# A convolution layer on Trainium2: kept low weight parts, seven taps from GpSimd to VectorE, and bias tables by three products instead of twelve

## The chip, the cores and the metric

The kernel runs on one core of a Trainium2 chip. Engines are named as in the profile: PE is TensorE, DVE is VectorE, ACT is ScalarE, POOL is GpSimd, SP is SyncE, whose queue issues most DMAs. The metric is the device time of one execution in microseconds (us), as the median of several runs.

## What is computed

A trunk of a convolution layer and an attention layer, each followed by a dense SwiGLU FFN, on 1024 tokens with 1024 channels in float32. The change lies in the convolution layer and in the table of position biases that attention uses later:

```
u = h @ w_pw1 + b_pw1
a, gate = split(u, 2)
u = a * sigmoid(gate)
u = depthwise_conv(u, w_dw, width 31, causal) + b_dw
u = silu(layernorm(u, ln_g, ln_b))
out = u @ w_pw2 + b_pw2
...
bias = bias_table[t5_bucket(dist * dilation)]
```

## The kernel before

The tokens are worked on in two halves of 512, h0 and h1. Channels lie on partitions, in eight chunks c of 128, so a tile is 128 x 512. Products in float32 are made of three products of rounded parts: `gemm` multiplies high weight by high data (L155), low weight by high data (L156) and high weight by low data (L157), eight times three matmuls for a tile. A tile is divided by `split`: ACT casts it to its high part (L127), and DVE or POOL subtracts that from it to get the low part (L128).

`conv_and_half_ffn` runs the convolution layer and the first FFN's half. `pw1_weights(c)` loads the two weight tiles of chunk c from `w1` (two DMAs of 512 KB on SP) and splits them. `glu(h, c)` makes the two products of the gate (L155 to L157), the sigmoid on ACT (L367) and the gated tile u on DVE (L374). The first half takes all eight chunks; chunks 5 to 7 do the second half too with the same weights. The chunks 0 to 4 of the second half load and split their weights again: 0 to 3 ahead of the convolution's end, 4 behind the layernorm in the program's text.

`conv(0)` is the convolution of width 31 for h0. A pair of chunks has 31 taps: `POOL_TAPS` of them are multiplied by ACT (L403, into the buffers m, of which there are two) and summed by POOL (L404), the rest are multiplied and summed by DVE into a bank of PSUM (L410, L412); a last addition on DVE joins the two (L422). The weights of the second half, the splits of L128 and the taps share DVE, POOL and ACT.

`layernorm(0)` follows: column sums on PE over the eight chunks (L434), subtraction of the mean on DVE (L436), squares on ACT (L457) and their column sums on PE (L458), square root on ACT (L460), reciprocal on DVE (L464), eight scalings on DVE (L468), Silu on ACT (L470), and a split into the pair y. `pw2` multiplies y by `w2`, whose eight weight tiles come through `weights` (DMA at L140), and adds into x. Then come the norm and the FFN of h0; the convolution of h1 runs beside that FFN and waits for its norm.

`bias_rows` makes the bias tables of the twelve heads: three groups of four. For each group a one-hot table is loaded (L603), and for each head one product on PE (L607) spreads its row over 128 partitions, ACT negates it (L609) and stores 192 KB to the memory `scratch` on its own queue (L610). Attention reads `scratch` much later, at about 1100 us.

The order of the instructions on each engine is found by the framework's scheduler from the program's order and its own model; what an engine does next is fixed when the kernel is built.

Of the kernel before, what the change touches and what calls it, by code (L numbers as in the profile page):

```python
# [17 lines left out]
P = 128  # L18
T = 1024
TH = 512  # L20
D = 1024
# [23 lines left out]

POOL_TAPS = ((11, 14, 15, 15), (10, 10, 9, 9))

# [38 lines left out]
@with_exitstack  # L86
def trunk(ctx, tc, xT, vecs, wdw, w1, w2, wqkv, wo, wg, wu, wd, rel, onehot, sel, outT, scratch):
    nc = tc.nc
# [49 lines left out]
    def weights(ap, n=D, into=None):  # L138
# [8 lines left out]
        return wh, wl  # L147

    def gemm(ps, w, xs, kt=DC, off=0):

        wh, wl = w
        for k in range(kt):
            sl = slice(off + k * P, off + (k + 1) * P)
            xh, xl = xs(k)
            nc.tensor.matmul(ps, wh[:, sl], xh, start=(k == 0), stop=False)  # L155
            nc.tensor.matmul(ps, wl[:, sl], xh, start=False, stop=False)  # L156
            nc.tensor.matmul(ps, wh[:, sl], xl, start=False, stop=(k == kt - 1))  # L157

# [13 lines left out]
    main = Scratch(tpool, "tmp", tpool, "ssq", aux_ps)  # L172


    marks = {}

# [142 lines left out]
    def conv_and_half_ffn():  # L319

        with ExitStack() as cs:
# [12 lines left out]

            def pw1_weights(c):

                t = slot([P, 2, 2, D])
                for i in range(2):
                    pw1_part(t, c, i, staging(), slice(0, D))
                return pw1_pairs(t)  # L340

            def staging():
# [8 lines left out]
            def pw1_pairs(t):  # L351
                return [(t[:, i, 0], t[:, i, 1]) for i in range(2)]

            def glu(h, c, hl, bc=None, w=None):

                wb, wa = w or pw1_weights(c)
                pb = mm_ps()
# [66 lines left out]
            def layernorm(h, sl, y):  # L424
# [42 lines left out]
                for c in range(DC):  # L467
                    nc.vector.tensor_tensor(out=vs[c], in0=vs[c], in1=br, op=ALU.mult)  # L468
                    t = sc.tmp()[:, :n]
                    nc.scalar.activation(  # L470
                        t,
                        vs[c],
                        AF.Silu,
                        bias=vec[:, V_LNB + c : V_LNB + c + 1],
                        scale=vec[:, V_LNG + c : V_LNG + c + 1],
                    )
                    split(t, yh[:, c, sl], yl[:, c, sl], nc.vector if c % 2 else nc.gpsimd)

# [40 lines left out]
            for c in range(DC):  # L519
                w = pw1_weights(c) if c else pw1_pairs(first)  # L520
                glu(0, c, ha, bc, w)
                if c == 0:
                    nc.sync.dma_start(wd_sb, wdw)
                if c in (1, 2):
                    for i in range(4):
                        load_x(1, (c - 1) * 4 + i)
                if c == NORM_B:
                    rms_into(hb, 1, V_MIX, sc=nsc)
                if c >= JOINT:
                    glu(1, c, hb, w=w)  # L530
# [7 lines left out]
            layernorm(0, whole, y)  # L538
            bias_rows()
            for c in range(LATE[0], LATE[1]):  # L540
                glu(1, c, hb)
            pw2(0, whole, y)
            for c in range(LATE[1], JOINT):
# [51 lines left out]
    def bias_rows():  # L595
# [5 lines left out]
        for g in range(NG):  # L601
            oh = tmp()[: NBK + 1, : 3 * P]
            nc.sync.dma_start(oh, onehot[g])  # L603
            for h in range(HPG):
                c = g * HPG + h
                ps = aux_ps()[:, : 3 * P]
                nc.tensor.matmul(ps, rb[:, c : c + 1].broadcast_to([NBK + 1, P]), oh, start=True, stop=True)  # L607
                br = tmp()[:, : 3 * P]
                nc.scalar.mul(br, ps, -1.0)  # L609
                nc.scalar.dma_start(scratch[g, h], br)  # L610

# [711 lines left out]
```

## Time and profile before

| | us |
|---|---|
| median of 3 runs | 2151.76 |
| runs | 2149.31, 2153.92, 2151.76 |
| the profiled execution | 2155.0 |
| its span in the trace | 2153.0 |
| PE busy | 2090.3 (97%) |
| DVE busy | 1361.7 (63%) |
| ACT busy | 845.2 (39%) |
| POOL busy | 550.0 (26%) |

Busy time is the time in which an engine works on an instruction. A share over the whole span is a mean of stages that have different limits, so it does not say what sets the time in a stage; the timeline of a stretch and what ended an engine's idle time do. The granted clock is a share of TensorE's full speed.

### The profile page before, as it was taken

How to read it: one execution, taken by the hardware profiler on the slowest of the kernel's cores; microseconds unless marked ns; L12 is line 12 of the kernel's file. 1: busy time of each engine (PE TensorE's matmuls, PEld its weight loads, DVE VectorE, ACT ScalarE, POOL GpSimd, SP SyncE). 2: the span in 40 equal slices, each digit the busy share in tenths (PEclk: the TensorE clock that was granted, in tenths of full speed). 3: DMA queues.
4: the chain of work that ended last, by engine and by line, in shares of the span. 5: the costliest groups of instructions: out<-in, count | busy, mean ns of one | idle time of the engine just before them, and what ended most of it. 6: DMA issues, size and time to landing. Idle time of an engine off the chain costs nothing.

```text
span 2153.0 us, 24602 instructions
## 1 busy us (share of the span) xinstructions
PE 2090.3 (97%) x9568; PEld 1686.9 (78%) x9568; DVE 1361.7 (63%) x1979; ACT 845.2 (39%) x1362; POOL 550.0 (26%) x336
## 2 busy tenths in 40 slices
PE   8998889999999999999999999999999999999997
PEld 6786578778887888888887777777888888888887
DVE  8998577998545433332562437489866666666665
ACT  6765656523423222212353434455322222222234
POOL 2998159922322222211231112130000000000003
PEclk9999989999999999999999999999999999999999
DMA  6111222223232222221231212112111111111112
GB/s 238 59 40 50 85 69 89 79 98 98 89 98 91 97 96 98 98 88 49 71 116 59 69 54 67 45 62 88 60 59 59 50 49 59 49 50 40 59 59 79
DMA packets 51320, 162.12 MB, mean 75 GB/s; under 512 B 5885, under 2 KB 11268, under 8 KB 51204
## 3 DMA queue, kind: packets, MB, share of 16 engines
q1 hardware_dynamic: 48900, 157.67, 22.2%
q10 hardware_dynamic: 2304, 2.88, 0.4%
q8 instruction: 75, 1.23, 0.2%
q14 instruction: 41, 0.34, 0.1%
HBM read 153.98 MB, written 6.55 MB: 75 GB/s over the span
## 4 chain that ended last, share of the span: by engine, by line
PE 76%; DVE 10%; POOL 9%; issue 3%; ACT 2%; DMA 1%; SPq 0%; POOLq 0%; DVEq 0%; ACTq 0%
PE mm L155 11%; PE mm L156 11%; PE mm L157 11%; POOL ap L404 7%; PE aux L155 6%; PE aux L156 6%; PE aux L157 6%; PE mm L1003 4%; PE mm L1001 4%; PE mm L1002 4%; DVE cacc L412 3%; PE nps L1001 2%; PE nps L1002 2%; PE nps L1003 2%; DVE slot L128 2%
## 5 line engine op out<-in xcount | busy, mean ns | idle before, releaser
L155 PE MATMUL mm<-slot,wh 128*128 128x512 f32 x1184 | 467.5, 395 | 5.3 <-DVE u L374 3.7
L156 PE MATMUL mm<-slot,wl 128*128 128x512 f32 x1184 | 466.4, 394 | 2.6 <-DVE wl L128 2.5
L157 PE MATMUL mm<-slot,wh 128*128 128x512 f32 x1184 | 464.0, 394 | 1.3 <-DVE slot L128 1.3
L128 POOL TENSOR_TENSOR wl<-ws,wh 128x1024 fp32r<-128x1024 f32 (+1 forms) x91 | 215.4, 2368 | 792.5 <-ACT wh L127 761.3
L127 ACT CAST wh<-ws 128x1024 fp32r<-128x1024 f32 (+1 forms) x190 | 195.6, 1030 | 337.2 <-PE mm L157 160.9
L155 PEld LDWEIGHTS mm<-slot,wh 128*128 128x128 f32 x1184 | 224.6, 190 | 57.5 <-issue 7.6
L156 PEld LDWEIGHTS mm<-slot,wl 128*128 128x128 f32 x1184 | 224.5, 190 | 51.9 <-DVE wl L128 3.8
L157 PEld LDWEIGHTS mm<-slot,wh 128*128 128x128 f32 x1184 | 224.0, 189 | 49.8 <-DVE slot L128 1.7
L404 POOL TENSOR_TENSOR ap<-ap,m 128x512 f32<-128x512 f32 x170 | 247.9, 1492 | 46.6 <-ACT m L403 46.6
L128 DVE TENSOR_TENSOR wl<-ws,wh 128x1024 fp32r<-128x1024 f32 (+1 forms) x99 | 131.5, 1329 | 151.1 <-ACT wh L127 150.9
L412 DVE SCALAR_TENSOR_TENSOR cacc<-u,wd_sb,cacc 128x512 f32<-128x512 f32 x288 | 198.8, 744 | 0.1
L128 POOL TENSOR_TENSOR slot<-ws,slot 128x1024 fp32r<-128x1024 f32 x2 | 4.8, 2407 | 638.9 <-ACT slot L127 638.9
L403 ACT ACTIVATE m<-u,wd_sb 128x512 f32<-128x512 f32 x170 | 121.6, 723 | 91.0 <-POOL ap L404 90.7
L155 PE MATMUL aux<-slot,wh 128*128 128x512 f32 x352 | 139.1, 395 | 7.7 <-DVE x L316 7.7
L1001 PE MATMUL mm<-slot,wp 128*128 128x512 f32 x352 | 137.6, 391 | 3.0 <-ACT wp L127 1.6
L156 PE MATMUL aux<-slot,wl 128*128 128x512 f32 x352 | 138.5, 393 | 0.8 <-DVE wl L128 0.5
L157 PE MATMUL aux<-slot,wh 128*128 128x512 f32 x352 | 138.4, 393 | 0.0
L1002 PE MATMUL mm<-slot,wp 128*128 128x512 f32 x352 | 137.6, 391 | 0.0
L1003 PE MATMUL mm<-slot,wp 128*128 128x512 f32 x352 | 137.0, 391 | 0.0
L127 ACT CAST wp<-ws 128x512 fp32r<-128x512 f32 x110 | 67.9, 620 | 142.2 <-PE mm L1003 58.2
L918 DVE TENSOR_TENSOR x<-aux,x 128x512 f32<-128x512 f32 x144 | 98.7, 688 | 35.3 <-PE aux L157 34.4
L128 DVE TENSOR_TENSOR slot<-tmp,slot 128x512 fp32r<-128x512 f32 x58 | 96.0, 1658 | 28.7 <-ACT slot L127 28.4
(269 smaller groups left out, 3820.4 us busy)
## 6 DMA issues: line engine op xcount, KB each, us to landing
ws<-wd SPq DMA_DIRECT2D x66, 512.0 KB, 3.5
ws<-wu SPq DMA_DIRECT2D x64, 512.0 KB, 3.5
ws<-wg SPq DMA_DIRECT2D x62, 512.0 KB, 3.5
ws<-w SPq DMA_DIRECT2D x40, 512.0 KB, 3.6
ws<-wqkv SPq DMA_DIRECT2D x34, 512.0 KB, 3.5
ws<-wo SPq DMA_DIRECT2D x16, 384.0 KB, 3.1
x<-xT SPq DMA_DIRECT2D x16, 256.0 KB, 6.3
scratch<-tmp ACTq DMA_DIRECT2D x12, 192.0 KB, 1.9
```

The lines of the kernel that those rows point to most:

```text
L127: a = nc.scalar.copy(hi, src)
L128: b = eng.tensor_tensor(out=lo, in0=src, in1=hi.bitcast(F32), op=ALU.subtract)
L155: nc.tensor.matmul(ps, wh[:, sl], xh, start=(k == 0), stop=False)
L156: nc.tensor.matmul(ps, wl[:, sl], xh, start=False, stop=False)
L157: nc.tensor.matmul(ps, wh[:, sl], xl, start=False, stop=(k == kt - 1))
L403: nc.scalar.activation(m, src(c, k), AF.Copy, scale=wk)
L404: nc.gpsimd.tensor_tensor(out=a, in0=a, in1=m, op=ALU.add)
L412: nc.vector.scalar_tensor_tensor(out=a if k or late else u[h, c][:, :TH], in0=src(c, k), scalar=wk, in1=b if k == nv - 1 else a, op0=ALU.mult,
L918: eng.tensor_tensor(out=out, in0=a, in1=b, op=op)
L1001: nc.tensor.matmul(ps, wh, xh, start=start and k == 0, stop=False, skip_group_check=not start)
L1002: nc.tensor.matmul(ps, wl, xh, start=False, stop=False, skip_group_check=not start)
L1003: nc.tensor.matmul(ps, wh, xl, start=False, stop=k == 3, skip_group_check=not start)
```

## The change

Four things change in `conv_and_half_ffn` and `bias_rows`.

- `POOL_TAPS` for h0 goes from (11, 14, 15, 15) to (11, 13, 12, 12) per pair of chunks: seven taps of two chunks, so fourteen products on ACT and sums on POOL, become fourteen instructions on DVE.
- A memory tensor `kept1` takes the low parts of the weights of chunks 0 to 4 (ten stores of 512 KB on SP). For h1 these chunks load the weight again, cast it on ACT, and load the low part from `kept1` and cast it on ACT too; the subtraction on DVE is gone there.
- In the layernorm of h0 the high part of y is a copy on DVE instead of a cast on ACT; the low part is a subtraction on DVE or POOL as before.
- `bias_rows` may start when the last product of glu(1, 4) is done. One product per group makes the rows of four heads, 32 partitions each, with a table `heads` that DVE writes first (one copy per group); DVE negates the result (three times); each head's 32 partitions go out four times, 48 KB each, on SP's queue: 48 stores.

```
@@ -43,7 +43,7 @@
 SKEW = 3 * P - 1
 
 
-POOL_TAPS = ((11, 14, 15, 15), (10, 10, 9, 9))
+POOL_TAPS = ((11, 13, 12, 12), (10, 10, 9, 9))
 
 
 LATE_SUM = ((0, 1, 2, 3), (0,))
@@ -154,7 +157,8 @@
             xh, xl = xs(k)
             nc.tensor.matmul(ps, wh[:, sl], xh, start=(k == 0), stop=False)
             nc.tensor.matmul(ps, wl[:, sl], xh, start=False, stop=False)
-            nc.tensor.matmul(ps, wh[:, sl], xl, start=False, stop=(k == kt - 1))
+            mm = nc.tensor.matmul(ps, wh[:, sl], xl, start=False, stop=(k == kt - 1))
+        marks["gemm"] = mm.ins
 
     def pairs(hl, sl=slice(None)):
         hi, lo = hl
@@ -332,12 +333,26 @@
             stage = ("ws", "ws", "wh", "wl", "wh", "wl", "wh", "wl")
             staged = [0]
 
-            def pw1_weights(c):
+            def pw1_weights(c, again=False):
+
 
                 t = slot([P, 2, 2, D])
                 for i in range(2):
-                    pw1_part(t, c, i, staging(), slice(0, D))
+                    ws = staging()
+                    if again:
+                        nc.sync.dma_start(ws, w1[c if i else DC + c])
+                        nc.scalar.copy(t[:, i, 0], ws)
+                        lo = staging()
+                        nc.sync.dma_start(lo, kept1[c, i])
+                        nc.scalar.copy(t[:, i, 1], lo)
+                    else:
+                        pw1_part(t, c, i, ws, slice(0, D))
+                        if c < JOINT:
+                            pw1_keep(t, c, i)
                 return pw1_pairs(t)
+
+            def pw1_keep(t, c, i):
+                nc.sync.dma_start(kept1[c, i], t[:, i, 1].bitcast(F32))
 
             def staging():
                 tag = stage[staged[0] % len(stage)]
@@ -353,7 +368,7 @@
 
             def glu(h, c, hl, bc=None, w=None):
 
-                wb, wa = w or pw1_weights(c)
+                wb, wa = w or pw1_weights(c, True)
                 pb = mm_ps()
                 gemm(pb, wb, pairs(hl))
                 pa = mm_ps()
@@ -474,7 +489,12 @@
                         bias=vec[:, V_LNB + c : V_LNB + c + 1],
                         scale=vec[:, V_LNG + c : V_LNG + c + 1],
                     )
-                    split(t, yh[:, c, sl], yl[:, c, sl], nc.vector if c % 2 else nc.gpsimd)
+                    if h == 0:
+                        nc.vector.tensor_copy(yh[:, c, sl], t)
+                        eng = nc.vector if c % 2 else nc.gpsimd
+                        eng.tensor_tensor(out=yl[:, c, sl], in0=t, in1=yh[:, c, sl].bitcast(F32), op=ALU.subtract)
+                    else:
+                        split(t, yh[:, c, sl], yl[:, c, sl], nc.vector if c % 2 else nc.gpsimd)
 
             def pw2(h, sl, y):
                 for d in range(DC):
@@ -520,6 +540,8 @@
                 w = pw1_weights(c) if c else pw1_pairs(first)
                 glu(0, c, ha, bc, w)
                 if c == 0:
+                    pw1_keep(first, 0, 0)
+                    pw1_keep(first, 0, 1)
                     nc.sync.dma_start(wd_sb, wdw)
                 if c in (1, 2):
                     for i in range(4):
@@ -536,9 +558,10 @@
                     touch(y)
             conv(0, range(4))
             layernorm(0, whole, y)
-            bias_rows()
             for c in range(LATE[0], LATE[1]):
                 glu(1, c, hb)
+            with tc.issue_after(marks["gemm"]):
+                bias_rows()
             pw2(0, whole, y)
             for c in range(LATE[1], JOINT):
                 glu(1, c, hb)
@@ -599,15 +622,20 @@
         nc.vector.memset(rb, 1.0)
         nc.sync.dma_start(rb[:NBK], rel)
         for g in range(NG):
-            oh = tmp()[: NBK + 1, : 3 * P]
+            both = tmp()[: NBK + 1]
+            oh, heads = both[:, : 3 * P], both[:, 3 * P :]
             nc.sync.dma_start(oh, onehot[g])
+
+            cols = rb[:, g * HPG : (g + 1) * HPG].unsqueeze(2).broadcast_to([NBK + 1, HPG, P // HPG])
+            nc.vector.tensor_copy(heads.rearrange("p (h r) -> p h r", h=HPG), cols)
+            ps = aux_ps()[:, : 3 * P]
+            nc.tensor.matmul(ps, heads, oh, start=True, stop=True)
+            br = tmp()[:, : 3 * P]
+            nc.vector.tensor_scalar(out=br, in0=ps, scalar1=-1.0, scalar2=None, op0=ALU.mult)
             for h in range(HPG):
-                c = g * HPG + h
-                ps = aux_ps()[:, : 3 * P]
-                nc.tensor.matmul(ps, rb[:, c : c + 1].broadcast_to([NBK + 1, P]), oh, start=True, stop=True)
-                br = tmp()[:, : 3 * P]
-                nc.scalar.mul(br, ps, -1.0)
-                nc.scalar.dma_start(scratch[g, h], br)
+                for i in range(HPG):
+                    n = P // HPG
+                    nc.sync.dma_start(scratch[g, h, i * n : (i + 1) * n], br[h * n : (h + 1) * n])
 
     def toeplitz(apool, g):
 
```

On PE, at the end of the layernorm's squares. L458, now L473, is the column sum of the squares; L607, now L632, the product of the biases; slot and wh, wl are the operands of pw2. Before:

```order
L458 MATMUL aux<-ctmp,ones 128x512
L607 MATMUL aux<-tmp,vec 128x384
L458 MATMUL aux<-ctmp,ones 128x512 x2
L607 MATMUL aux<-tmp,vec 128x384
L458 MATMUL aux<-ctmp,ones 128x512
L607 MATMUL aux<-tmp,vec 128x384
L458 MATMUL aux<-ctmp,ones 128x512
L607 MATMUL aux<-tmp,vec 128x384
L458 MATMUL aux<-ctmp,ones 128x512 x2
L607 MATMUL aux<-tmp,vec 128x384 x2
L458 MATMUL aux<-ctmp,ones 128x512
L607 MATMUL aux<-tmp,vec 128x384 x6
```

The change:

```order
L473 MATMUL aux<-ctmp,ones 128x512
L632 MATMUL aux<-tmp 128x384
L473 MATMUL aux<-ctmp,ones 128x512 x2
L632 MATMUL aux<-tmp 128x384
L473 MATMUL aux<-ctmp,ones 128x512 x5
L158 MATMUL mm<-slot,wh 128x512
L159 MATMUL mm<-slot,wl 128x512
L158 MATMUL mm<-slot,wh 128x512
L159 MATMUL mm<-slot,wl 128x512
L632 MATMUL aux<-tmp 128x384
```

Twelve bias products have become three; the third of them stands behind the first four products of pw2. All products of the last projection, glu(1, 4), are now ahead of these rows, and 32 of their 48 ahead of the last column sum of L449 (L434 before).

On DVE, behind the squares. L464 and L468, now L479 and L483, are reciprocal and scaling; L374, now L389, is the gated product of glu(1, 4); L630 writes the table of heads and L634 negates the result; L493 and L495 are high and low part of y. Before:

```order
L422 TENSOR_TENSOR u<-cacc,ap 128x512 x2
L436 SCALAR_TENSOR_TENSOR u<-aux,u 128x512 x8
L464 RECIPROCAL csv<-csv 128x512
L468 TENSOR_TENSOR u<-u,csv 128x512 x8
L374 SCALAR_TENSOR_TENSOR u<-mm,vec,tmp 128x512
L128 TENSOR_TENSOR slot<-ctmp,slot 128x512
L374 SCALAR_TENSOR_TENSOR u<-mm,vec,tmp 128x512
L128 TENSOR_TENSOR slot<-ctmp,slot 128x512 x3
```

The change:

```order
L634 TENSOR_SCALAR tmp<-aux 128x384
L630 COPY tmp<-vec 33x128
L634 TENSOR_SCALAR tmp<-aux 128x384
L479 RECIPROCAL csv<-csv 128x512
L630 COPY tmp<-vec 33x128
L483 TENSOR_TENSOR u<-u,csv 128x512 x8
L389 SCALAR_TENSOR_TENSOR u<-mm,vec,tmp 128x512
L493 CAST slot<-ctmp 128x512 x2
L389 SCALAR_TENSOR_TENSOR u<-mm,vec,tmp 128x512
L495 TENSOR_TENSOR slot<-ctmp,slot 128x512
L493 CAST slot<-ctmp 128x512 x2
L634 TENSOR_SCALAR tmp<-aux 128x384
```

The scalings stand together as before, but behind the third copy of heads, which writes into a buffer that the stores of the first group's rows read; the copies of y stand between the last negations and the gate.

On SP, from the weights of pw2 on. L140 loads those weights, L627 a one-hot table, L638 stores bias rows:

```order
L140 DMA ws<-w 128x1024 x5
L627 DMA tmp<-onehot 33x384 x2
L638 DMA scratch<-tmp 32x384 x32
L627 DMA tmp<-onehot 33x384
L638 DMA scratch<-tmp 32x384 x16
L140 DMA ws<-w 128x1024 x3
```

The stores of a group stand behind its negation on DVE, and the third group's one-hot table behind 32 of them; before, the stores were on ACT's queue. The loads of the last three weight tiles of pw2 come behind all 48.

## Rows read from the trace of the kernel before

**Rows 1.** Page: busy time by engine, the chain by engine and by line.
```profile
PE 2090.3 (97%) x9568; PEld 1686.9 (78%) x9568; DVE 1361.7 (63%) x1979; ACT 845.2 (39%) x1362; POOL 550.0 (26%) x336
...
PE 76%; DVE 10%; POOL 9%; issue 3%; ACT 2%; DMA 1%; SPq 0%; POOLq 0%; DVEq 0%; ACTq 0%
PE mm L155 11%; PE mm L156 11%; PE mm L157 11%; POOL ap L404 7%; PE aux L155 6%; PE aux L156 6%; PE aux L157 6%; PE mm L1003 4%; PE mm L1001 4%; PE mm L1002 4%; DVE cacc L412 3%; PE nps L1001 2%; PE nps L1002 2%; PE nps L1003 2%; DVE slot L128 2%
```

**Rows 2.** Windows: stretch, length, busy us of PE, PEld, DVE, ACT, POOL, clock, DMA, GB/s.
```profile
144.00:200.00 56.00, 55.97 (x240) 44.67 (x239) 53.59 (x69) 38.52 (x56) 51.80 (x36) 1.00 0.09 30
200.00:207.00 7.00, 0.55 (x3) 0.12 (x1) 5.36 (x7) 3.73 (x5) 7.00 (x6) 0.82 0.38 141
207.00:213.00 6.00, 5.38 (x12) 3.34 (x13) 1.94 (x4) 0.00 (x0) 1.06 (x1) 0.64 0.03 13
213.00:239.00 26.00, 19.83 (x44) 7.49 (x44) 14.60 (x19) 18.62 (x33) 1.76 (x1) 0.86 0.26 95
```

**Rows 3.** Waits of PE: us in total, times, longest.
```profile
PE aux L434 <- DVE u L422: 7.1, 1, 7.1
```

**Rows 4.** Timeline of POOL: start, length, line, count, idle before and its releaser.
```profile
139.52 5.52 POOL L404 TENSOR_TENSOR ap<-ap,m 128x512 f32<-128x512 f32 x4
...
189.11 18.96 POOL L404 TENSOR_TENSOR ap<-ap,m 128x512 f32<-128x512 f32 x12 [0.84 <-ACT m L403]
```

**Rows 5.** Timeline of DVE, same columns.
```profile
165.39 1.22 DVE L128 TENSOR_TENSOR slot<-ws,slot 128x1024 fp32r<-128x1024 f32 x1
...
187.50 1.86 DVE L128 TENSOR_TENSOR slot<-ws,slot 128x1024 fp32r<-128x1024 f32 x1
...
208.10 0.69 DVE L422 TENSOR_TENSOR u<-cacc,ap 128x512 f32<-128x512 f32 x1 [0.53 <-POOL ap L404]
212.32 4.88 DVE L436 SCALAR_TENSOR_TENSOR u<-aux,u 128x512 f32<-128x512 f32 x8 [3.53 <-PE aux L434]
228.56 3.35 DVE L464 RECIPROCAL csv<-csv 128x512 f32<-128x512 f32 x1 [11.37 <-ACT csv L460]
231.95 5.97 DVE L468 TENSOR_TENSOR u<-u,csv 128x512 f32<-128x512 f32 x8
```

**Rows 6.** Timeline of PE, same columns.
```profile
188.33 3.59 PE L434 MATMUL aux<-u,ones 128*128 128x512 f32 x8
...
225.63 1.12 PE L458 MATMUL aux<-ctmp,ones 128*128 128x512 f32 x2
...
230.70 4.38 PE L607 MATMUL aux<-tmp,vec 33*128 33x384 f32 x8 [2.46 <-DMA tmp<-onehot]
238.73 0.77 PE L155 MATMUL mm<-slot,wh 128*128 128x512 f32 x1 [3.66 <-DVE u L374]
239.30 0.63 PE L156 MATMUL mm<-slot,wl 128*128 128x512 f32 x1
239.72 0.63 PE L157 MATMUL mm<-slot,wh 128*128 128x512 f32 x1
```

**Rows 7.** Groups by line and form, 0 to 240: busy us, mean ns, idle before.
```profile
L404 POOL TENSOR_TENSOR ap<-ap,m 128x512 f32<-128x512 f32 x102 | 146.4, 1471 | 41.6 <-ACT m L403 41.6
...
L412 DVE SCALAR_TENSOR_TENSOR cacc<-u,wd_sb,cacc 128x512 f32<-128x512 f32 x130 | 90.3, 743 | 0.1
...
L128 DVE TENSOR_TENSOR slot<-ws,slot 128x1024 fp32r<-128x1024 f32 x24 | 36.7, 1542 | 1.9 <-ACT slot L127 1.8
L127 ACT CAST slot<-ws 128x1024 fp32r<-128x1024 f32 x24 | 24.1, 1042 | 4.7 <-PE mm L157 4.7
```

**Rows 8.** Timeline of ACT, same columns as group 4.
```profile
227.84 0.69 ACT L460 ACTIVATE csv<-aux,vec 128x512 f32<-128x512 f32 x1
```

**Rows 9.** Issues on SP, start and length; landing of the stores of L610.
```profile
2.59 0.43 SPq L111 DMA_DIRECT2D x<-xT  x1
3.06 0.43 SPq L348 DMA_DIRECT2D ws<-w  x1
...
DMA to landing us min/median/max: 1.9/1.9/2.0
```

More of the change, by code (lines that the diff above doesn't have):

```diff
@@ L86, in trunk @@
 @with_exitstack
-def trunk(ctx, tc, xT, vecs, wdw, w1, w2, wqkv, wo, wg, wu, wd, rel, onehot, sel, outT, scratch):
+def trunk(ctx, tc, xT, vecs, wdw, w1, w2, wqkv, wo, wg, wu, wd, rel, onehot, sel, outT, scratch, kept1):
     nc = tc.nc
@@ L147, in weights @@
         return wh, wl
+    marks = {}
     def gemm(ps, w, xs, kt=DC, off=0):
@@ L172, in trunk @@
     main = Scratch(tpool, "tmp", tpool, "ssq", aux_ps)
-    marks = {}
     def colsum(st, src, n):
@@ L1317 @@
     aps.append(nc.dram_tensor("scratch", (NG, HPG, P, 3 * P), F32, kind="Internal").ap())
+    aps.append(nc.dram_tensor("kept1", (JOINT, 2, P, D), F32, kind="Internal").ap())
     with tile.TileContext(nc, schedule_with_timeline_sim=True) as tc:
```

## The prediction

> **What bounds the kernel now.** The first thing to read is the page's head. TensorE (PE) is busy for 97% of the span, and 76% of the chain that ended last is on PE; but 9% of it is on POOL and 10% on VectorE (DVE), and the two largest lines of those are the convolution's taps, L404 and L412 [rows 1]. So there is a stage in which PE isn't what sets the end. The stretches show where: PE is busy for 55.97 of 56 us before 200, for 0.55 of the 7 us from 200 to 207, and then works at a granted clock of 0.64 and 0.86 of full speed, a mix of its two levels of 1.2 and 2.4 GHz, up to 239 [rows 2]. The waits of PE name the cause of the hole: 7.1 us at the column sum L434, for the DVE's last sum of the convolution's two halves [rows 3]. POOL has no gap but 0.84 us between its batches of taps, and its last twelve end at 208.07 [rows 4]. The last DVE sum waits 0.53 us for POOL and ends at 208.79; the layernorm starts behind it [rows 5]. From there to the first product of the second projection (pw2) at 238.73 [rows 6] everything is a chain through PE, DVE and ACT. Both DVE (53.59 of 56) and POOL (51.80 of 56) are full before 200 [rows 2], so the end of the convolution, and not PE, sets the start of pw2, and behind that the rest of the program.
>
> **The change, part by part.** *End of the convolution.* Fourteen taps leave ACT and POOL and come to DVE; ten splits of weights leave DVE; ten casts come to ACT. DVE: fourteen taps at 90.3 / 130 = 0.69 us are 9.7 us, ten splits at 1.54 us are 15.4 us [rows 7]. DVE was idle 2.4 us in 144 to 200, 1.6 us in 200 to 207 [rows 2] and 0.5 us before the last sum, 4.5 us in all. If nothing makes it wait it ends at 208.8 - 4.5 - 15.4 + 9.7 = 198.6; I take 199. POOL: 44 taps stood behind 139.52, in six batches of which the first and the last are shown [rows 4]; with fourteen fewer in all, 30 are left, at 1.47 us [rows 7] at most 44.1, and at the 1.38 of the batch at 139.52 41.4. ACT now does casts four in a row where it did two. There are two buffers of products for POOL, so each such stop costs the 0.84 us it cost before and up to two casts of 1.04 us more, 2.9 us, five times: 14.6. That gives 195.5 to 198.2; I take 197. Bounds: with only the old 0.84 per stop 185 for POOL, so DVE's 198 decides; with 1.58 us a tap, as in the last batch, and the full stops 201.5, and with one more cast in each stop to wait for 207. So the end moves from 208.8 to 199, **-9.8 us** (bounds -11 and -2).
>
> *Column sums.* They ended 3.5 us behind the last DVE sum: DVE waited that long for L434 [rows 5], because PE came out of the hole at the low clock and had five products of the projection between. In the new order the last projection's gemm (1,4) stands around them: 32 of its products ahead, 16 behind. PE finishes the former at about 196, so it waits 3 us and not 7, and the one sum that is left, at 3.59 / 4 = 0.9 us (two matmuls to a channel) [rows 6], and 0.3 us of handing over make 1.2. **-2.4 us** (0 if the clock falls anyway).
>
> *Squares.* From the first subtraction to ACT's square root it took 227.84 - 212.32 = 15.5 us [rows 5, 8]. Before: six bias products stood between the squares' column sums. Now: sixteen products of the projection, two bias products. Sixteen at 56 / 240 = 0.233 us [rows 2] are 3.7 (this hides the first subtraction and square), eight sums of squares at the same 0.9 us are 7.2, two bias products at some 0.8 (the eight matmuls at 230.70, four products, took 4.38 with their gaps [rows 6]) 1.6, and 1.1 from the end of the last sum, at 226.75, to the square root [rows 6, 8]: 13.6. **-1.9 us**.
>
> *Scaling and y.* Square root 0.69 and reciprocal 3.35 stay [rows 5, 8]. Then the first pw2 product came 6.8 us behind the reciprocal's end, behind four of the eight scalings and a cast on ACT. Now eight scalings run in a row, 5.97 us [rows 5], then 0.66 us for the gate and 0.3 to 0.6 for the copy of y on DVE: 7.2. **+0.4 us**.
>
> *Clock.* Ahead of pw2 PE is now idle for about 12 us where eight bias products stood before. Before, the clock was 0.86 in 213 to 239 [rows 2], and the first pw2 products came 0.42 us apart [rows 6]. Another stretch like that costs 0 to 3 us; I take **+1 us**.
>
> *Costed at nothing.* The ten kept stores take 0.47 us of SP each [rows 9]; if every one held up a load that PE waits for, they would cost 4.7 us, but POOL and DVE, not the loads, set the end of the convolution [rows 4, 5], and their cover is that load. The ten loads of kept parts fall in a stretch where the DMA is busy 9% [rows 2]. Twelve ACT copies and stores go: ACT waits for others there. The 48 stores on SP: issue pitch 0.47 us [rows 9]. The third bias copy on DVE stands between the reciprocal and the scalings and waits for the first sixteen stores; two copies behind it wait in the same way, and the third bias product stands ahead of nearly all of pw2 on PE. Counted from the end of the column sums, the first tile's product can start at 3.7 + 0.9 = 4.6; with 2 us for it and its negation, 16 x 0.47 for the stores and 2 for a landing [rows 9] they are done at 16.1, and the reciprocal at 13.6 + 0.7 + 3.4 = 17.7: hidden by 1.6 us. Thirty-two, with 1.9 us for the second tile's copy, product and negation, are done at 25.5; the y copies that they could stop come, behind the scalings, the gate and the first four copies and low parts, at about 28.8: hidden by 3.3 us. The third one-hot table stands behind those stores and lands at the same 25.5; its product is wanted behind four products of pw2, at about 26: hidden by 0.5 us only. What goes on behind 300 waits for the norm behind pw2 as before, and its work is the same.
>
> The sum: -9.8 - 2.4 - 1.9 + 0.4 + 1.0 = -12.7 us. The profiled execution took 2155.0 us, 2.0 above its span and 3.2 above the median of the runs, 2151.76. So 2142.3 for such an execution, and 2139.1 for the median.
>
> A rule of the page "GPSIMD Engine Reference" of the Trainium skill (section 1, Specifications) says that POOL's interfaces to SBUF are shared with DVE's instructions of two SBUF inputs or in a two-port mode. The rows agree for two inputs: a DVE split took 1.22 us at 165.39, in a gap of POOL, and 1.86 at 187.50 beside it [rows 5]. By that rule the eight new copies of y on DVE, if they run in such a mode, would hold up POOL's four low parts of y; at 0.64 us each the sum would be -10.1 and not -12.7.
>
> **The rivals.** *A, POOL starves behind the casts (0.12).* Ten casts more go through ACT, which feeds POOL through two buffers; POOL's gaps are already all ACT's, 41.6 us up to 240 [rows 7]. If each row of four casts stops POOL for its whole length, the end comes at 204 and not 199 and PE falls to the low clock again: -5 for the end, -2 for the squares, nothing else, 2145. Against it: POOL's load falls by fourteen taps.
>
> *B, the small stores take the place of the wait (0.09; slower).* A tile of 192 KB was one store on ACT's queue, which landed in 1.9 us [rows 9]; now there are sixteen of 48 KB on SP. If they don't overlap, the third product on PE, and the rest of pw2 behind it, waits until 32p + 10.5 us against 26, p being the pitch. Up to p = 0.48 nothing shows, at p = 0.88 the gain is gone, and at p = 2.0, a landing for each, pw2 comes 48 us late: 36 us slower, 2188. For it: the landing row. Against it: SP issued 0.47 apart to several destinations while landings took longer.
>
> The page "DMA: Bandwidth & Descriptors" of the Trainium skill (Bandwidth, Measured) says to batch transfers and that under 64 KB they are ruled by descriptors; it speaks for B, and no row of this trace has a store of that size.
>
> *C, no change (0.08).* Something else holds the convolution's end, a kept part that comes late or a DVE order that waits for POOL's pair by pair, or the gain is lost in a clock that stays low: within 4 us of 2151.8.
>
> *D, more than 20 us (0.05).* DVE and POOL both speed up without the ten splits (1.22 against 1.86 [rows 5]), the end comes at 195 (-14), PE has no hole and runs sums and squares at the full clock (-6) and the first of pw2 too (-1.5): about 2130.
>
> **How the numbers follow.** The forecast has 0.66 and gives 8 to 20 us, 2132 to 2144 around 2139.1. With A the range goes to 2148; this leaves out B, C and part of D. A measurement of this kernel tells 0.2%, 4.3 us, from no change. Faster: 0.66 and most of A and D, 0.81; same: C and the edge of A, 0.09; slower: B and the edge of C, 0.10.
>
> **What would show it.** Right: the wait at the column sum for DVE falls from 7.1 to about 3 us, POOL's last tap at about 197, the first pw2 product at about 225, no wait of DVE on stores, everything behind 300 earlier by the same 13 us. Wrong: ten stops of POOL of 3 us or more (A); DVE copies or PE's third bias product that wait for a DMA of scratch or of the one-hot table (B); a first pw2 product at 235 or later (C). If the first pw2 product comes early and the end doesn't, the time was given back behind 300, which no row here foretells.

## The result, and the profile after

The changed kernel took 2142.33 us as the median of 4 runs (2139.41 to 2143.35), the kernel before in the same comparison 2152.53; the ratio is 0.9949 with an interval of 0.9938 to 0.9961, that is 8 to 13 us less. The forecast was 2139.1, in a range of 2132 to 2148. The profiled execution has a span of 2140.7 us, 12.3 less than before.

The page of the changed kernel: busy time by engine, and the chain.

```profile
PE 2079.0 (97%) x9550; PEld 1681.0 (79%) x9550; DVE 1358.1 (63%) x1997; ACT 831.7 (39%) x1336; POOL 526.9 (25%) x322
...
PE 79%; DVE 9%; POOL 7%; issue 3%; ACT 2%; DMA 1%; SPq 0%; DVEq 0%; POOLq 0%; ACTq 0%
```

PE is busy for 11 us less, with 18 matmuls fewer, and POOL's share of the chain fell from 9% to 7% [rows 1]. The stretches (columns as in [rows 2]):

```profile
144.00:200.00 56.00, 56.00 (x239) 44.70 (x238) 51.26 (x75) 38.89 (x50) 36.09 (x28) 1.00 0.38 124
200.00:207.00 7.00, 7.00 (x25) 4.27 (x24) 5.41 (x10) 1.86 (x3) 0.00 (x0) 1.00 0.00 0
207.00:213.00 6.00, 6.00 (x15) 2.04 (x14) 0.70 (x3) 3.38 (x6) 0.00 (x0) 1.00 0.38 100
213.00:227.00 14.00, 3.80 (x8) 1.75 (x7) 11.74 (x16) 6.41 (x10) 1.38 (x2) 0.71 0.30 78
227.00:240.00 13.00, 13.00 (x46) 9.97 (x45) 6.96 (x10) 3.75 (x6) 3.78 (x3) 0.78 0.23 61
```

PE no longer stands still at 200 to 207. Its hole now lies at 213 to 227, in front of pw2, and the low clock behind that: 0.71 and 0.78. POOL is busy for 36.09 us of the 56 before 200 where it was 51.80 [rows 2].

DVE and POOL at the end of the convolution and in the layernorm (start, length, count, idle before and its releaser):

```profile
195.41 0.69 DVE L437 TENSOR_TENSOR u<-cacc,ap 128x512 f32<-128x512 f32 x1
...
201.09 4.87 DVE L451 SCALAR_TENSOR_TENSOR u<-aux,u 128x512 f32<-128x512 f32 x8 [4.87 <-PE aux L449]
...
214.78 3.35 DVE L479 RECIPROCAL csv<-csv 128x512 f32<-128x512 f32 x1 [5.00 <-ACT csv L475]
...
218.17 4.90 DVE L483 TENSOR_TENSOR u<-u,csv 128x512 f32<-128x512 f32 x8
...
226.43 0.43 DVE L493 CAST slot<-ctmp 128x512 fp32r<-128x512 f32 x1 [0.33 <-ACT ctmp L485]
227.13 1.35 DVE L493 CAST slot<-ctmp 128x512 fp32r<-128x512 f32 x1 [0.28 <-ACT ctmp L485]
```

```profile
171.47 7.55 POOL L419 TENSOR_TENSOR ap<-ap,m 128x512 f32<-128x512 f32 x6 [2.76 <-ACT m L418]
...
186.88 6.73 POOL L419 TENSOR_TENSOR ap<-ap,m 128x512 f32<-128x512 f32 x4 [1.99 <-ACT m L418]
```

The last DVE sum starts at 195.41 and not at 208.10, and waits for nobody [rows 5]. POOL's last tap ends at 193.61. The taps of the batch at 171.47 take 7.55 / 6 = 1.26 us each where the last batch of before took 1.58 [rows 4]; the last four of the change, with DVE's splits of the weights of pw2 beside them, still take 1.68. Five of POOL's six stops behind 139.52 are 2 to 3.3 us long, not 0.84. Then comes a surprise: the first subtraction waits 4.87 us for the column sum, longer than the 3.53 of before. PE shows why, and ACT's square root stands below it:

```profile
196.41 1.02 PE L449 MATMUL aux<-u,ones 128*128 128x512 f32 x2
...
200.04 1.02 PE L449 MATMUL aux<-u,ones 128*128 128x512 f32 x2
...
204.57 1.02 PE L473 MATMUL aux<-ctmp,ones 128*128 128x512 f32 x2
...
224.12 0.79 PE L158 MATMUL mm<-slot,wh 128*128 128x512 f32 x1 [10.20 <-DVE slot L493]
...
226.12 1.65 PE L632 MATMUL aux<-tmp 33*128 33x384 f32 x2
```

```profile
214.06 0.69 ACT L475 ACTIVATE csv<-aux,vec 128x512 f32<-128x512 f32 x1
```

Between the last two column sums, 196.41 and 200.04, PE does twelve products of the projection, and between the last column sum and the first sum of squares, 204.57, sixteen more.

By stages, the two profiled executions compare so. A norm is read at its reciprocal on DVE:

| | before | after | moved by |
|---|---|---|---|
| first norm | 57.40 | 55.81 | -1.6 |
| last sum of the convolution ends | 208.79 | 196.10 | -12.7 |
| first subtraction | 212.32 | 201.09 | -11.2 |
| square root starts | 227.84 | 214.06 | -13.8 |
| first product of pw2 | 238.73 | 224.12 | -14.6 |
| norm behind pw2 | 290.43 | 279.24 | -11.2 |
| norm ahead of the attention stage | 1096.05 | 1085.75 | -10.3 |
| norm behind the attention stage | 1435.66 | 1422.41 | -13.2 |
| span | 2153.0 | 2140.7 | -12.3 |

The rows of the norm behind pw2, before and after:

```profile
290.43 0.18 DVE L209 RECIPROCAL rs<-sd 128x4 f32<-128x4 f32 x1 [2.25 <-ACT sd L207]
```

```profile
279.24 0.18 DVE L210 RECIPROCAL rs<-sd 128x4 f32<-128x4 f32 x1 [2.26 <-ACT sd L208]
```

So 14.6 us were there at the start of pw2, and pw2 gave 3.4 of them back. Of the 14.6, 1.6 were there at the first norm already. They are no gain of the change: over all profiles that norm came at 55.1 to 58.3 us with the kept stores and at 55.1 to 57.8 without them.

### The profile page after: what moved, and what is told of

Same layout as the page of the kernel before. It is cut to its first block, busy times and chain, and to the rows that moved or that the text cites. A ratio compares the mean times of both kernels' runs of the same rounds, so it can differ in the third digit from the quotient of the medians.

```text
span 2140.7 us, 24625 instructions
## 1 busy us (share of the span) xinstructions
PE 2079.0 (97%) x9550; PEld 1681.0 (79%) x9550; DVE 1358.1 (63%) x1997; ACT 831.7 (39%) x1336; POOL 526.9 (25%) x322
## 4 chain that ended last, share of the span: by engine, by line
PE 79%; DVE 9%; POOL 7%; issue 3%; ACT 2%; DMA 1%; SPq 0%; DVEq 0%; POOLq 0%; ACTq 0%
PE mm L158 12%; PE mm L160 12%; PE mm L159 12%; PE aux L158 6%; PE aux L160 6%; PE aux L159 6%; POOL ap L419 5%; PE mm L1031 4%; PE mm L1029 4%; PE mm L1030 4%; DVE cacc L427 2%; PE nps L1029 2%; PE nps L1030 2%; PE nps L1031 2%; PE att L768 1%
## 5 line engine op out<-in xcount | busy, mean ns | idle before, releaser
L158 PE MATMUL mm<-slot,wh 128*128 128x512 f32 x1184 | 467.5, 395 | 11.8 <-DVE slot L493 10.2
L419 POOL TENSOR_TENSOR ap<-ap,m 128x512 f32<-128x512 f32 x156 | 224.7, 1474 | 55.2 <-ACT m L418 55.1
L427 DVE SCALAR_TENSOR_TENSOR cacc<-u,wd_sb,cacc 128x512 f32<-128x512 f32 x302 | 207.8, 743 | 0.1
L418 ACT ACTIVATE m<-u,wd_sb 128x512 f32<-128x512 f32 x156 | 111.0, 722 | 77.4 <-POOL ap L419 77.2
L127 ACT CAST wp<-ws 128x512 fp32r<-128x512 f32 x110 | 67.8, 621 | 147.8 <-PE mm L1031 55.2
```

What stands on the lines that cost most here:

```text
L127: a = nc.scalar.copy(hi, src)
L418: nc.scalar.activation(m, src(c, k), AF.Copy, scale=wk)
L419: nc.gpsimd.tensor_tensor(out=a, in0=a, in1=m, op=ALU.add)
L427: nc.vector.scalar_tensor_tensor(out=a if k or late else u[h, c][:, :TH], in0=src(c, k), scalar=wk, in1=b if k == nv - 1 else a, op0=ALU.mult,
```

## Experiments

Every run is set against the kernel before on the same chip; the ratios and their intervals are those comparisons. The differences in us in the text are between medians. The median of the kernel before differed by up to 1.6 us between the comparisons (2152.04 to 2153.65), so where a difference between two runs is small, the ratios are given beside it.

### Which part brings it: five runs that undo one or two parts

Taps back (POOL_TAPS alone):

```
-POOL_TAPS = ((11, 13, 12, 12), (10, 10, 9, 9))
+POOL_TAPS = ((11, 14, 15, 15), (10, 10, 9, 9))
```

> The change with the fourteen taps back on ACT and POOL (11, 14, 15, 15). My theory: the convolution's end is the later of two chains, DVE's and POOL's, and the kept weights alone only shorten DVE's. POOL has 14 taps of 1.26 us more (17.6 us) and stops of 2.7 us between its batches, so its last tap comes at about 212 instead of 193.6, the first product of pw2 at about 236 instead of 224.1, and the time is 2152 to 2156, no better than before the change. Rival: the two parts act each by itself, the kept weights bring about half of the gain alone: 2146 to 2148, with the last tap at about 203.

Measured: 2151.42 us, ratio 0.9991 (0.9982 to 1.0).

Kept parts out, seven taps on DVE:

```
-                wb, wa = w or pw1_weights(c, True)
+                wb, wa = w or pw1_weights(c)
...
-                        if c < JOINT:
-                            pw1_keep(t, c, i)
...
-                    pw1_keep(first, 0, 0)
-                    pw1_keep(first, 0, 1)
```

> The change without the kept low parts: the second half's weights are split on DVE again, no stores and no loads of kept parts. My theory: DVE, with 14 taps more and its ten splits of 1.2 to 1.9 us back, ends the convolution alone, at about 210 instead of 196.1; POOL's stops fall back to 0.84 us and its last tap comes at about 185. First product of pw2 at about 235, time 2151 to 2155. Rival: the taps bring about half of the gain alone: 2146 to 2148.

Measured: 2152.51 us, ratio 1.0001 (0.9993 to 1.001). With both edits at once:

> The change without the kept low parts and with the fourteen taps back on ACT and POOL: only the new bias products and the copies of y are left. My theory: DVE and POOL are then as full as in the kernel before and the convolution ends at 207 to 210, as it did with either part alone; the rest of the change brings little without them, 2149 to 2152. Together with the two runs that undo one part each, this says whether the two parts only gain together (this run like those two, the change 10 us under all three). Rival: each part brings its own half, and this run is some 10 us above those two.

Measured: 2147.14 us, ratio 0.9976 (0.9966 to 0.9985), below both forecasts. The timelines of POOL and DVE at the end of the convolution, with the taps back:

```profile
185.65 24.28 POOL L419 TENSOR_TENSOR ap<-ap,m 128x512 f32<-128x512 f32 x18 [1.66 <-ACT m L418]
```

```profile
208.74 0.69 DVE L437 TENSOR_TENSOR u<-cacc,ap 128x512 f32<-128x512 f32 x1 [14.78 <-POOL ap L419]
209.96 0.69 DVE L437 TENSOR_TENSOR u<-cacc,ap 128x512 f32<-128x512 f32 x1 [0.53 <-POOL ap L419]
```

without the kept parts, DVE:

```profile
212.18 0.69 DVE L435 TENSOR_TENSOR u<-cacc,ap 128x512 f32<-128x512 f32 x1
```

and with neither, DVE, then ACT's square root:

```profile
205.74 0.69 DVE L435 TENSOR_TENSOR u<-cacc,ap 128x512 f32<-128x512 f32 x1 [0.53 <-POOL ap L417]
...
209.60 4.87 DVE L449 SCALAR_TENSOR_TENSOR u<-aux,u 128x512 f32<-128x512 f32 x8 [3.04 <-PE aux L447]
```

```profile
220.61 0.69 ACT L473 ACTIVATE csv<-aux,vec 128x512 f32<-128x512 f32 x1
```

With the kept parts alone DVE stands idle for 14.78 us and waits for POOL, which has all its taps and longer stops: the end comes at 210.6. With the taps alone POOL is done at 185.9, and DVE ends at 212.9. With both it is 196.1, with neither 206.4. Without the kept parts the first product of pw2 comes at 242.21 and not at about 235: the clock stood at 0.50 from 208 at the latest to 229 there, through the column sums and the squares, so that run pays for the low clock on top of the late end. In times (ratios in brackets):

| | splits on DVE | kept parts |
|---|---|---|
| taps on POOL | 2147.1 (0.9976) | 2151.4 (0.9991) |
| taps on DVE | 2152.5 (1.0001) | 2142.3 (0.9949) |

By the medians either part alone makes the kernel 4 to 5 us slower and both together 5 us faster; by the ratios it is 3 and 5 us slower and 6 faster. The intervals of the kept parts alone and of neither part just touch, so it is clear that the kept parts alone bring nothing, and less clear that they cost. That confirms the two chains, of which the later one counts. It also shows what neither theory for the last run had: with neither part, the kernel is still 6.5 us faster than before by the medians, 5 by the ratio (3 to 7). That gain belongs to the bias products (and, at most, the copies of y), which the next two runs take apart.

Old bias products, with their ACT copies and stores, in their old place (`bias_rows` of the kernel before, called behind `layernorm`):

> The change with the twelve bias products, their ACT copies and twelve stores on ACT's queue, in the place they had before. My theory: four more products of 0.84 us and as many ACT copies of 0.5 us stand between the sums of squares, so the square root comes 3 to 5 us later, at 217 to 219, and the time is 2145 to 2148. Rival: PE is idle for 10 us ahead of pw2 anyway and the bias products cost nothing: 2141 to 2143.

Measured: 2145.87 us, ratio 0.9963 (0.995 to 0.9977), 3.5 us more than the change; by the ratios it is 3, and the intervals overlap. ACT's square root and PE's first product of pw2:

```profile
217.49 0.69 ACT L475 ACTIVATE csv<-aux,vec 128x512 f32<-128x512 f32 x1
```

```profile
228.22 0.80 PE L158 MATMUL mm<-slot,wh 128*128 128x512 f32 x1 [3.94 <-ACT tmp L382]
```

The square root is 3.4 us later, as expected. The loss of 4.1 us at the first product of pw2 is down to 0.8 at the norm (280.06 against 279.24); the clock was back at full 3.6 us behind that product here (at 231.8) and 8.5 us behind it in the change (at 232.6), so pw2 had less to do at the low one. The rest of the 3.5 lies in the attention stage of this profile, where the clock fell (see the last runs); how much of it belongs to the bias products stays open.

High part of y by a cast on ACT, `split` for both halves as before:

> The change with the high part of y by a cast on ACT again. My theory: the DVE copies bring little; the eight scalings ahead of them keep the first copy until 223.65, so with the cast on ACT the first product of pw2 comes at 221 to 223 instead of 224.1, but ACT needs 0.81 + 0.62 us per chunk; the time is within 2 us of the change, 2140 to 2144. Rival (what the change does): a Silu with its cast in turn on ACT holds pw2 up, 2145 to 2148.

Measured: 2140.66 us, ratio 0.9943 (0.993 to 0.9955). The first product comes at 221.00, 3.1 us sooner, but the time can't be told from the change's. The copies on DVE bring nothing that can be told; they wait behind the eight scalings.

### Why less came out than the start of pw2 promised

The sixteen and twelve products around the column sums had to be tried. The second half of glu(1, 4) is held back behind the last sum of squares, where PE idles for 10.2 us:

```
-                gemm(pa, wa, pairs(hl))
+                with ExitStack() as held:
+                    if hold is not None:
+                        marks["first"] = marks["gemm"]
+                        held.enter_context(tc.issue_after(hold))
+                    gemm(pa, wa, pairs(hl))
...
-                        nc.tensor.matmul(ps, ones, sq, start=(c == 0), stop=(c == DC - 1))
+                        marks["squares"] = nc.tensor.matmul(ps, ones, sq, start=(c == 0), stop=(c == DC - 1)).ins
...
-                glu(1, c, hb)
-            with tc.issue_after(marks["gemm"]):
+                glu(1, c, hb, hold=marks["squares"])
+            with tc.issue_after(marks["first"]):
                 bias_rows()
```

> The change with the second half of the last projection, 24 products of glu(1, 4), held back behind the last sum of squares; the bias products may start behind its first half. My theory: 16 products in front of the squares put the square root 3 to 4 us off while PE idles for 10.2 us later; held back, they run in that idle time. Square root at about 210 instead of 214.06, first product of pw2 at about 220 instead of 224.12, and less low clock behind it, since the idle time is halved: 2136 to 2139. Rival: DVE (subtractions) and ACT (squares) set the pace and PE's products were hidden, or the held half delays the gate on DVE ahead of the copies of y: 2141 to 2144.

Measured: 2134.06 us, ratio 0.9916 (0.9902 to 0.9929), 8.3 us less than the change (7 by the ratios, whose intervals lie apart); the lowest median of all. PE and ACT in it:

```profile
197.77 1.02 PE L453 MATMUL aux<-u,ones 128*128 128x512 f32 x2
200.23 1.13 PE L477 MATMUL aux<-ctmp,ones 128*128 128x512 f32 x2 [1.44 <-ACT ctmp L476]
...
219.89 0.80 PE L158 MATMUL mm<-slot,wh 128*128 128x512 f32 x1 [4.75 <-DVE slot L497]
```

```profile
209.83 0.69 ACT L479 ACTIVATE csv<-aux,vec 128x512 f32<-128x512 f32 x1
```

The last column sum is at 197.77 and the first sum of squares at 200.23 (204.57 in the change), so the square root comes 4.2 us sooner and the first product of pw2 too. PE's products in front were the bound, not DVE or ACT. At the norm behind pw2 the lead over the change is 5.8 us (273.44 against 279.24). The rest of the 8.3 arises behind it and is not explained here.

Then the third bias product, which stood in pw2. All one-hot tables are loaded ahead of the stores:

```
+        tabs = []
         for g in range(NG):
-            both = tmp()[: NBK + 1]
+            tabs.append(tmp()[: NBK + 1])
+            nc.sync.dma_start(tabs[g][:, : 3 * P], onehot[g])
+        for g in range(NG):
+            both = tabs[g]
             oh, heads = both[:, : 3 * P], both[:, 3 * P :]
-            nc.sync.dma_start(oh, onehot[g])
```

> The change with the three one-hot tables loaded ahead of all stores, so that the third bias product stands among the sums of squares and not in pw2. My theory: the product took 1.58 us at the low clock in pw2 and takes 0.85 at the full clock before: pw2 takes 1.6 us less, the square root comes 0.9 later, 2140 to 2142, not to be told from the change. Rival (the third product's wait for its table is what lengthens pw2 by 3.4 us): 2138 to 2139.

Measured: 2138.96 us, ratio 0.994 (0.9927 to 0.9954); the interval overlaps the change's, so the times do not settle it. The profiles say more. PE in the same stretch, the change first, then this kernel (columns as in [rows 2]):

```profile
226.00:232.00 6.00, 6.00 (x13) 3.93 (x13) 4.75 (x8) 3.45 (x5) 2.55 (x2) 0.50 0.17 44
```

```profile
226.00:232.00 6.00, 6.00 (x23) 4.80 (x22) 4.72 (x7) 3.73 (x5) 2.59 (x2) 0.79 0.36 93
```

The clock is at its lower level, 1.2 GHz (0.50), over the whole stretch in the change, and back at the upper one for most of it here; 13 products against 23. From the first product of pw2 to the addition of its third tile it took 257.29 - 238.73 = 18.6 us before, 245.73 - 224.12 = 21.6 in the change, 244.11 - 224.56 = 19.6 here (DVE, the addition's rows):

```profile
245.73 0.75 DVE L504 SCALAR_TENSOR_TENSOR x<-mm,vec,x 128x512 f32<-128x512 f32 x1 [0.71 <-PE mm L160]
```

```profile
244.11 0.75 DVE L504 SCALAR_TENSOR_TENSOR x<-mm,vec,x 128x512 f32<-128x512 f32 x1
```

The table was not waited for: the product at 226.12 follows its neighbour at once. What it cost was its 1.58 us and a longer stretch at the low clock, the rival's size but not its cause.

The other profiles agree. From the first product of pw2 to the norm behind it took 51.7 to 52.1 us where no bias product stood in pw2 (before, old bias products, one-hot tables first, kept parts out), 52.5 to 53.6 where the third one stood in pw2 behind the return of the clock (taps back, neither part, held half), and 55.1 and 55.2 in the two profiles of the change. The clock was back 3.3 to 5.0 us after the first product in the first seven, and 8.5 and 9.6 us after it in the change. So, as an estimate from these rows, about 1 of the 3.4 us is the product itself and about 2 the longer stretch at the low clock. Why one such product goes with it is not shown. (The runs with the cast on ACT wait for y inside pw2 and the one with 96 stores for a weight, so they are left out here.)

All three edits together, and the first and third:

> The change with three edits: the second half of glu(1, 4) held back behind the squares, the one-hot tables first, and the high part of y by a cast on ACT. My theory: the gains add up where they lie on one chain; first product of pw2 at about 217 and the time 2133 to 2137. Rival: pw2 starts earlier and gives it back at the low clock, as the change did with 3.4 us: 2138 to 2141.

> The change with the second half of glu(1, 4) held back behind the squares and the high part of y by a cast on ACT; the one-hot tables as in the change, so the third bias product stands in pw2. My theory: first product of pw2 at about 217, as with all three edits; the third bias product lies behind the point where the clock is back at full, so it costs 0.9 us there as it would among the squares: 2132 to 2136, the same as the other two. Rival: the bias product prolongs the low clock here as it did in the change, 2136 to 2139.

Measured: 2134.6 us (0.992, 0.9906 to 0.9933) and 2134.69 us (0.9913, 0.9897 to 0.9929). The first products of pw2 come at 216.21 and 218.25, but PE then waits for y (1.16 us for POOL at 218.11, for one), and neither can be told from the held half alone. In the held half alone the third bias product lies at 226.52, behind the return of the clock.

### The small stores

Each store cut in two (24 KB, 96 of them):

> The change with every bias store cut in two: 96 stores of 24 KB on SP instead of 48 of 48 KB. My theory: each store costs SP its 0.46 us, so SP is held 22 us longer; the loads of the last three weight tiles of pw2, which stand behind the stores, are issued at about 258 instead of 242, and PE waits for them: 2145 to 2150. Rival: the stores are hidden with so much to spare that twice their number costs nothing: 2141 to 2144.

Measured: 2139.33 us, ratio 0.9941 (0.9929 to 0.9954): my size was wrong. SP's issues, and PE's one wait:

```profile
206.53 30.76 SPq L639 DMA_DIRECT2D scratch<-tmp  x64
...
243.86 16.46 SPq L639 DMA_DIRECT2D scratch<-tmp  x32
```

```profile
266.44 0.50 PE L159 MATMUL mm<-slot,wl 128*128 128x512 f32 x1 [0.76 <-DVE wl L128]
```

The stores do hold SP longer, 30.76 and 16.46 us. But the scheduler moved two of the three weight loads between them, so only the eighth tile comes late, its load issued at 260.43, and PE waits 0.76 us for its low part, not 5. It also moved the third bias product nearly seventy products further into pw2, to 242.33, behind the low clock. By the addition of the third tile this profile was 2.8 us quicker behind the first product than the change's (242.44 - 223.60 = 18.8 against 21.6); at the norm nothing of that is left (55.2 against 55.1 us behind the first product). Of the loss 0.9 us is the third bias product and 0.8 the wait, so twice the stores cost at most about 2 us there. The interval of this run overlaps the change's, so the times do not tell the two apart. For the change itself, the stores were issued in 0.42 us and landed in 1.6:

```profile
L638 SPq DMA_DIRECT2D scratch<-tmp x48: 303/419/422, 207.0 to 235.8; - x48
...
DMA to landing us min/median/max: 1.6/1.6/1.6
```

### How far one profile can be read

The changed kernel and the kernel with three edits were profiled a second time.

> The changed kernel again, for a second profile. In the attention stage PE waits 1.28 us once for DVE; in the profiles of before, of the old bias products and of the three edits the clock then fell to 0.5 for about 6 us, in the others not. If that hangs on the program, it does not fall here either, as in the first profile; if it falls in some executions and not in others of one program, this one may fall, and its attention stage is then 3 us longer (339.6 us between the two norms around it instead of 336.7).

> The kernel with three edits again, for a second profile and more times: 2133 to 2136. Its first profile had the clock's fall in the attention stage. If that hangs on the program, it is here again; if not, it may be missing, and the span is then some 3 us shorter than 2135.6.

Measured: 2141.51 us (one run, span 2139.7) and 2135.61 us. In the attention stage of the three edits, PE had the same wait for DVE of 1.3 us in both executions. In the first profile the clock fell behind it, in the second not (windows):

```profile
1396.00:1398.00 2.00, 2.00 (x5) 1.61 (x6) 1.92 (x3) 0.67 (x2) 0.93 (x1) 0.50 0.00 0
```

```profile
1400.00:1402.00 2.00, 1.93 (x8) 1.12 (x7) 2.00 (x6) 0.62 (x1) 0.44 (x1) 1.00 0.50 164
```

Between the two norms around it the stage took 339.6 us (1074.27 to 1413.88) and 336.7 (1080.05 to 1416.71). So in this program the drop comes in some executions and not in others. The profile of before has it, both profiles of the change do not (339.6 against 336.7 us), and, other than the expectation says, the profiles with the one-hot tables first and with 96 stores have it too. So some 3 of the 12.3 us between the spans may be no effect of the change; whether the change makes the drop rarer stays open. The medians, 10.2 apart, rest on several executions each.

## Why the prediction was right, and where not

*End of the convolution* (-9.8): right in its mechanism, both chains shorten and only together, as the two runs with one part each show. The end moved by 12.7 between the profiles and by 10.3 against the run with neither part. Counted from the first norm (57.40 before, 55.81 in the change, 55.09 with neither part) it moved by 11.1 against both; the other 1.6 us are a difference between executions at the start, which no term of the forecast meant. DVE ended at 196.1 (199 forecast), POOL at 193.6 (197): most of its stops grew to 2.7 as priced (2.9), and its 29 taps behind 141.79 took 38.3 / 29 = 1.32 us on average and not 1.38 to 1.47.

*Column sums* (-2.4): wrong, they came to +1.5: 201.09 - 196.10 = 5.0 us, where there had been 3.5 and 1.2 was forecast. The step that failed is "PE finishes the former at about 196". PE did not wait for DVE at all: it started the sum of chunk seven at 196.41 with twelve products still to do; the end of the convolution had passed PE, and PE became the bound there. The 196 stands on no row, and the profile of before could have told it: there PE starts the same 48 products at 191.36 and takes 0.23 us for each, so 32 of them and a column sum of 0.9 us are through at about 199.6; in the change it was 200.0. (Between the last two column sums of before stood four products, not the five of the prediction.)

```profile
191.36 0.79 PE L155 MATMUL mm<-slot 128*128 128x512 f32 x1
```

So the 3 us by which the convolution ended sooner than forecast could bring nothing: the first subtraction was forecast for 200.2 and came at 201.09, when PE was through. In the second profile of the change the term was +0.3 (199.20 - 195.39 = 3.8 us), wrong in the same direction. The held half shows it: with most of those products out of the way the first subtraction came 198.82 - 196.60 = 2.2 us behind the end.

*Squares* (-1.9): from the first subtraction to the square root it took 214.06 - 201.09 = 13.0 us against 15.5 before, -2.5. *Scaling and y* (+0.4): from the reciprocal's end to the first product it took 6.0 us and not 7.2; eight scalings took 4.90 us where they had 5.97 beside POOL [rows 5]. That is -0.8.

*Clock* (+1): mis-sized, it was +3.4, and part of it was a thing that the prediction had named as a wait and not as work: the third bias product inside pw2. It waited for nothing, but took 1.58 us at the low clock, and the low clock lasted longer than in any profile without a bias product at this place. (The "eight bias products" of the prediction are eight matmuls, four products, as its own paragraph on the squares says.)

The terms as measured: -1.6 ahead of the first norm, then -11.1 + 1.5 - 2.5 - 0.8 + 3.4, in sum -11.1 at the norm (-11.2 before rounding), and -10.2 in the times. The forecast was -12.7. The end of the convolution, the squares and the scaling brought more than forecast, the column sums and the clock less, and that these errors nearly cancel is luck. "Everything behind 300 earlier by the same 13 us" did not hold as it stands: the lead was 11.2 us at the norm and 10.3 at 1096, and came back to 13.2 in the attention stage, where the profile of before has the drop of the clock. The prediction also did not see how much the bias products and the copies of y bring on their own: 5 to 6.5 us with the old convolution. With the new one it is about 3 for the bias products, not clear of the noise, and nothing that can be told for the copies.

*A* (POOL starves behind the casts): the stops grew, to 2 to 3.3 us, near the forecast's 2.9 and short of the four casts (4.2 us) that this rival needs, and fourteen taps less outweighed them; with the taps back they cost 4.3 us (3 by the ratios). *B* (stores): pitch 0.46 us, and no wait in the change. Its mechanism does exist: without the kept parts DVE waited 4.61 and 3.54 us for the stores and PE 5.32 for the third one-hot table, but DVE then waited 3.12 us for the square root and PE 3.27 for y all the same, so it cost nothing there.

```profile
225.42 0.56 DVE L630 TENSOR_SCALAR tmp<-aux 128x384 f32<-128x384 f32 x1 [4.61 <-DMA scratch<-tmp]
```

The rule of "DMA: Bandwidth & Descriptors" of the Trainium skill (Bandwidth, Measured) on transfers under 64 KB, measured there for loads issued from GpSimd, did not come into it in the change, since the time lay in issuing (0.46 us for 48 KB, 0.48 for 24 KB) and was hidden. *C* and *D* did not happen.

By the rule of "GPSIMD Engine Reference" of the Trainium skill (section 1, Specifications), as the prediction read it, the copies of y were to hold up POOL's low parts of y. The trace shows the contention and shows it on the other side: POOL's four low parts took 1.27 to 1.31 us, and the DVE copies 0.43 alone and 1.35 beside one of them (226.43 and 227.13 above). PE waited for no part of y behind its first product, so the sum did not change by it.

## What to carry to other kernels

Where two engines feed one point, moving work between them pays only if both get shorter: here either half of the move cost 3 to 5 us and both together won 5 to 6. When a wait is shortened, look at what the waiting engine was doing meanwhile, since its filler work becomes the next bound; put that filler into the next hole (7 to 8 us here, where the whole change brought 10). A lone instruction in the first us after a hole can go with a longer stretch at the low clock and then costs more than its length: an estimated 3 us here, of which 1 was its own. And a term such as "PE is through at about 196" needs a row: the profile of before had one.

## What the runs showed of the hardware that was not expected

In the attention stage PE had a wait of about 1.3 us at one place in every profile; behind it the granted clock stood at 0.50 for 3 to 10 us in five of the fourteen profiles and stayed at 1.00 in the others, and two executions of one program differed in this. Ahead of pw2, PE stopped at 213.9 in the change, and the clock fell at 219.0; in the second profile of the change PE stopped at 212.0 and the clock fell at 214.7. In the first it was at 0.50 from the first product of pw2 at 224.12 until 232.6, 8.5 us, with a bias product of 33 rows behind the first four products; without that product it was back sooner: from 238.73 to 242.0 before, from 219.89 to 224.9 with the held half. Two executions of one program also differed by 2.3 us at the first norm already (55.49 and 57.82), and by 4.7 at the norm behind pw2 (270.77 and 275.46), while their times lay within 0.5 us (2137.42 and 2136.94).
